# An encoder trunk laid out feature by token: x resident, two token groups, contiguous weight tiles through a ring, and the 31-tap convolution as four concurrent 32-column matmuls

## Chip, cores, metric

The kernel runs on the 8 cores of one Trainium2 chip. Each core does half of one prompt (2048 of 4096 tokens) and one sample of 32 tokens, with all weights. The metric is device time of the slowest core in microseconds (us). In some executions one die (cores 0 to 3 or 4 to 7), sometimes both, showed a lower granted TensorE clock, and the time was longer: one run of the kernel before took 3632.04 us with all eight cores at 0.794 to 0.799, where its fast runs took 3263 to 3300.

## The reference, cut to what matters

```python
D_MODEL, D_INNER, CHUNK, MLP_BLOCK = 1024, 2048, 64, 128
for i in range(DEPTH):                      # four layers, each with its own mixer
    shift, scale, gate = ada_modulation(c, w_ada[i], b_ada[i])
    h = rms_norm(x, g_norm[i]) * (1.0 + scale) + shift
    # kind 0: u, v, z = split(h @ w_in_a);  v = layer_norm(gelu(v))     (gelu on u too)
    #         y = u * chunk_mlp_mix(v, w_s_a, b_s_a)    mixes positions in blocks of 128
    # kind 1: bg, cg, hv, z = split(h @ w_in_b);  y = bg * conv3(cg * hv)
    # kind 2: a, ag, z = split(h @ w_in_c);  y = silu(layer_norm(conv31(a * sigmoid(ag)) + b))
    # kind 3: pv, z = split(h @ w_in_d);  y = (pool(pv) - pv) @ w_pool_d (per group) * scale
    out = (y * silu(z)) @ w_out             # 2048 -> 1024
    x = x + gate * out
return rms_norm(x, g_final), v_rows, conv_b_new, conv_c_new, pool_new
```

The convolutions are depthwise and causal; a core needs some tokens ahead of its half (the halo), and the last rows of each mixer's input are outputs too.

## The kernel before

x lies token by feature (128 tokens on the partitions). h, the input of every projection, lies feature by token. So each layer normalises a block of 128 tokens, transposes it on TensorE and moves it out of PSUM:

```python
def h_post(bi, bl, lt):
    ...
        for kc in range(8):
            dstp = ptA[:, kc, 0:n] if kc < 4 else ptB[:, kc - 4, 0:n]
            ins = h.transpose(out=dstp, in_=xn[:, kc * 128:(kc + 1) * 128], identity=identb[0:n, 0:n])
    ...
    for kc in range(4):        # VectorE: scale and shift while leaving PSUM
        s.op("dve", lambda h, kc=kc: h.tensor_scalar(out=hT[:, kc, c0:c0 + n], in0=ptA[:, kc, 0:n], ...
    for kc in range(4, 8):     # ScalarE: the other half
        s.op("act", lambda h, kc=kc: h.activation(out=hT[:, kc, c0:c0 + n], in_=ptB[:, kc - 4, 0:n], ...
```

The tokens of a core (2176 with halo, and the sample) are worked off in three passes through all four layers, each with its own load of every weight; tiles of 256 columns come out of row-major weights in 1 KB runs:

```python
ST_DEFS = [
    dict(b0=0, nb=6, ncols=768, ep=768, sample=False),
    dict(b0=6, nb=6, ncols=768, ep=768, sample=False),
    dict(b0=12, nb=5, ncols=704, ep=640, sample=True),
]
...
def fetch_in(l, col0):         # one of 16 slots of 1 MB of f32, kept as bf16
    s.dma("pool", "rs%d" % i, v, w_in[l].rearrange("(kc p) n -> p kc n", p=128)[:, :, col0:col0 + 256], ...
```

conv31 builds 28 diagonal 128 x 128 matrices per chunk of 128 channels on GpSimd and runs 28 full matmuls over the shifted input; three taps are left to ScalarE and VectorE:

```python
dg = ...                                    # diag(w[k]) for 28 taps
for (c0, n, b, bo) in nts:                  # 512 and 256 columns
    for k in range(NTD, 31):
        ins = h.matmul(bank(b)[:, bo:bo + n], lhsT=dg[:, k - NTD, :], rhs=G[:, c0 + k:c0 + k + n], start=(k == NTD), stop=(k == 30))
```

The v stage of layer 0 works off 128 tokens at a time: projection (front), LayerNorm statistics, vn (the normalised v, by ScalarE), mixing matmuls and 16 evictions from PSUM (back). The evictions are cut in two, with the statistics of the next block between them:

```python
    evac(0, 8)
    return lambda: evac(8, 16)
...
for bi, bl in enumerate(blocks):
    ctx = v_front(bi, bl)
    tail = v_back(*prevb) if prevb is not None else None
    v_stats(bi, bl, ctx)
    if tail is not None:
        tail()
```

Of the kernel before, what the change touches and what calls it, by code (L numbers as in the profile page):

```python
# [13 lines left out]
EPS = 1e-6  # L14

class Sched:
# [11 lines left out]
    def _deps(self, eng, reads, writes):  # L28
        waits = {}

        def add(sv):
            if sv is None:
                return
            sname, v = sv
            if v > waits.get(sname, 0):
                waits[sname] = v

        for k in reads:
            r = self.res.get(k)
            if r is not None:  # L40
                add(r[0])
        for k in writes:
            r = self.res.get(k)
            if r is not None:
                add(r[0])
                for sname, v in r[1].items():
                    add((sname, v))
        out = []
        for sname, v in waits.items():
            if self.seen[eng].get(sname, 0) >= v:  # L50
                continue
            self.seen[eng][sname] = v
            out.append((sname, v))
        return out
# [10 lines left out]
    def op(self, eng, fn, reads=(), writes=()):  # L65
        ro = getattr(self, "ring_out", None)
        if ro:
            for k in reads:
                ro.discard(k)
# [76 lines left out]
def build_program():  # L146
    nc = bass.Bass("TRN2", target_bir_lowering=False)

# [6 lines left out]
    xp = din("xp", [2176, D])  # L155
    xsm = din("xsm", [32, D])
    st_b = din("st_b", [2, E])
    st_c = din("st_c", [30, E])
    st_d = din("st_d", [15, E])
    cvec = din("cvec", [2, D])  # L160
    maskc_d = din("maskc", [128, 1])
    invc_d = din("invc", [128, 64])
    w_ada = din("w_ada", [4, D, 3 * D])
    b_ada = din("b_ada", [4, 3 * D])
    g_norm = din("g_norm", [4, D])
    w_in = [din("w_in_a", [D, 3 * E]), din("w_in_b", [D, 4 * E]), din("w_in_c", [D, 3 * E]), din("w_in_d", [D, 2 * E])]
    w_out = [din("w_out_a", [E, D]), din("w_out_b", [E, D]), din("w_out_c", [E, D]), din("w_out_d", [E, D])]
    prm9 = din("prm9", [9, E])
    w_conv_c = din("w_conv_c", [31, E])
    w_s_a = din("w_s_a", [8, 128, 128])  # L170
    b_s_a = din("b_s_a", [8, 128])
    w_pool = din("w_pool_d", [4, 512, 512])
    g_final = din("g_final", [1, D])
    ln_a_gb = din("ln_a_gb", [2, E])

    yp = dout("yp", [2048, D])
    ysm = dout("ysm", [32, D])
    vrows = dout("vrows", [32, E])
    o_cb_p = dout("cb_p", [2, E]); o_cb_s = dout("cb_s", [2, E])
    o_cc_p = dout("cc_p", [30, E]); o_cc_s = dout("cc_s", [30, E])  # L180
    o_pd_p = dout("pd_p", [15, E]); o_pd_s = dout("pd_s", [15, E])

    s = Sched(nc)
    TOTAL = 53000
    big = nc.alloc_sbuf_tensor("big", [128, TOTAL], F32)
    off = [0]

    def carve(nw):
        v = big[:, off[0]:off[0] + nw]
        off[0] += nw  # L190
        assert off[0] <= TOTAL, off[0]
        return v

    def v3(v, a):
        return v.rearrange("p (a b) -> p a b", a=a)

    X = v3(carve(6 * 1024), 6)
    XS = X[:, 5, :]
    hT = v3(carve(3072).bitcast(BF16), 8)
    ysT_raw = carve(6144)  # L200
    ysT = v3(ysT_raw.bitcast(BF16), 16)
    AUX_raw = carve(6400)
    AUX = v3(AUX_raw.bitcast(BF16), 16)
    RING = carve(16 * 1024)
    Traw = [carve(800) for _ in range(4)]
    gateP = [carve(1024), carve(1024)]
    gateS = carve(1024)
    dscr = [carve(128), carve(128)]
    scTb = v3(carve(8).bitcast(BF16), 8)
    gf_bc = carve(1024)  # L210
    biasT = v3(carve(2048), 16)
    biasT_s = v3(carve(512), 16)
    WsT = v3(carve(512).bitcast(BF16), 8)
    WsT_s = v3(carve(128).bitcast(BF16), 8)
    identb = carve(64).bitcast(BF16)
    identf = carve(128)
    onesf = carve(128)
    onesb = carve(64).bitcast(BF16)
    prmT = v3(carve(16 * 9), 16)
    wccT = v3(carve(16 * 32), 16)  # L220
    stT = v3(carve(16 * 48), 16)
    hist = v3(carve(16 * 48), 16)
    outS = v3(carve(16 * 48), 16)
    gnT = v3(carve(32), 8)
    badaT = v3(carve(96), 24)
    cT = v3(carve(16), 8)
    scT = v3(carve(16), 8)
    modT = carve(4 * 48)
    gsT = carve(4 * 16)
    stat = carve(64)  # L230
    maskc = carve(1)
    invc = carve(64)
# [7 lines left out]
    PS = nc.alloc_psum_tensor("ps", [128, 4096], F32)  # L240

    def bank(b):
        return PS[:, b * 512:(b + 1) * 512]

    def bk(*bs):
        return ["bk.%d" % b for b in bs]

    def Tf(i, n=800):
        return Traw[i][:, 0:n]

    def Tb(i, n=1600):
        return Traw[i].bitcast(BF16)[:, 0:n]

    def Tk(*idx):
        return ["T.%d" % i for i in idx]

    Tcat = big[:, Traw[0].offset - big.offset:Traw[0].offset - big.offset + 3200] if False else None

    t0_off = 6 * 1024 + 1024 + 3072 + 6144 + 6400 + 16 * 1024
    stage = big[:, t0_off:t0_off + 3200]  # L260
    Tpair01 = big[:, t0_off:t0_off + 1600]

    s.op("pool", lambda h: h.memset(identf, 0.0), writes=["identf"])
    s.op("pool", lambda h: h.affine_select(out=identf, in_=identf, pattern=[[-1, 128]], compare_op=ALU.not_equal,
                                           fill=1.0, base=0, channel_multiplier=1), reads=["identf"], writes=["identf"])
    s.op("dve", lambda h: h.tensor_copy(out=identb, in_=identf), reads=["identf"], writes=["identb"])
    s.op("dve", lambda h: h.memset(onesf, 1.0), writes=["onesf"])
    s.op("dve", lambda h: h.memset(onesb, 1.0), writes=["onesb"])
    s.op("dve", lambda h: h.memset(stat[:, 0:63], 0.0), writes=["stat_init"])
    s.op("dve", lambda h: h.memset(stat[:, 63:64], -0.5), writes=["neghalf"])  # L270
    s.op("dve", lambda h: h.memset(hist.rearrange("p a b -> p (a b)"), 0.0), writes=["hist"])
    s.dma("sp", "su_m", maskc, maskc_d, writes=["maskc"])
    s.dma("sp", "su_i", invc, invc_d, writes=["invc"])
    s.dma("sp", "su_g", gf_bc, g_final.partition_broadcast(128), writes=["gf_bc"])

    def load_rows_T(src, R, C, dst3, dkey, rp=32):
        nch = C // 128
        s.dma("sp", "su_st", stage[0:R, 0:C], src, writes=Tk(0, 1, 2, 3))
        pst = v3(bank(0)[:, 0:nch * rp], nch)

        def f(h):
            ins = None
            for c in range(nch):
                ins = h.transpose(out=pst[:, c, 0:R], in_=stage[0:R, c * 128:(c + 1) * 128], identity=identf[0:R, 0:R])
            return ins
        s.op("pe", f, reads=Tk(0, 1, 2, 3) + ["identf"], writes=bk(0))
        s.op("dve", lambda h: h.tensor_copy(out=dst3[:, :, 0:R], in_=pst[:, :, 0:R]), reads=[], writes=bk(0) + [dkey])

    load_rows_T(cvec, 2, D, cT, "cT")
    load_rows_T(g_norm, 4, D, gnT, "gnT")  # L290
    load_rows_T(b_ada, 4, 3 * D, badaT, "badaT", rp=4)
    load_rows_T(prm9, 9, E, prmT, "prmT")
    load_rows_T(w_conv_c, 31, E, wccT, "wccT")
    load_rows_T(st_b, 2, E, stT[:, :, 0:2], "stT")
    load_rows_T(st_c, 30, E, stT[:, :, 2:32], "stT")
    load_rows_T(st_d, 15, E, stT[:, :, 32:47], "stT")
    s.op("act", lambda h: h.activation(out=scT.rearrange("p a b -> p (a b)"), in_=cT.rearrange("p a b -> p (a b)"), func=AF.Silu),
         reads=["cT"], writes=["scT"])

    wsI = v3(stage[:, 0:1024], 8)  # L300
    s.dma("sp", "su_st", wsI, w_s_a.rearrange("g i j -> i g j"), writes=Tk(0, 1, 2))
    ps_w = v3(PS[:, 0:1024], 8)

    def f_ws_s(h):
        ins = None
        for g in range(8):
            ins = h.transpose(out=ps_w[0:32, g, 0:32], in_=wsI[0:32, g, 0:32], identity=identf[0:32, 0:32])
        return ins
    s.op("pe", f_ws_s, reads=Tk(0, 1, 2) + ["identf"], writes=bk(0, 1))
    s.op("dve", lambda h: h.tensor_copy(out=WsT_s[0:32, :, :], in_=ps_w[0:32, :, 0:32]), reads=[], writes=bk(0, 1) + ["WsT_s"])  # L310
    s.op("dve", lambda h: h.memset(wsI[0:64, :, 64:128], 0.0), reads=[], writes=Tk(0, 1, 2))

    def f_ws(h):
        ins = None
        for g in range(8):
            ins = h.transpose(out=ps_w[:, g, :], in_=wsI[:, g, :], identity=identf)
# [719 lines left out]
```

## Time and profile before

| | before |
|---|---|
| time, median of 3 | 3263.55 us (3263.26 to 3263.99) |
| cores in the profiled run | 3211.7 to 3272.4 us, clock 0.917 to 0.926 |
| matmuls on TensorE | 17058, busy 82% of the span |

The lines that the prediction rests on are quoted in it below. Three more views are needed for the comparison. First the waits of TensorE (who waited on which line, for whom; us in total, times, longest):

```profile
PE ps L547 <- ACT big L531: 126.2, 32, 18.2
PE ps L390 <- DMA big<-w_ada: 52.0, 7, 13.9
...
PE ps L672 <- ACT big L621: 18.8, 9, 2.3
```

L547 are the transposes of the norm, waiting for ScalarE's statistics and scaled rows: 126 us, the largest single item. L390 are the conditioning matmuls, waiting for weights. L672 are the mixing matmuls of the v stage: they wait 18.8 us for ScalarE (L621, its GELU) and, by a line not shown, 32.3 us for VectorE's evictions (L678).

Second, VectorE in one block of that stage. L678 are evictions, L631 to L643 the statistics (columns: start, us, engine, line, operation, output and inputs, shapes, count, and in brackets the idle time before it):

```profile
1301.06 1.26 DVE L678 SCALAR_TENSOR_TENSOR big<-ps,big 128x128 bf16<-128x128 f32 x3
1302.24 0.15 DVE L631 TENSOR_TENSOR big<-big 128x1 f32<-128x1 f32 x1
...
1304.25 0.16 DVE L643 SCALAR_TENSOR_TENSOR big<-big 128x1 f32<-128x1 f32 x1 [0.80 <-POOL big L641]
1304.33 3.54 DVE L678 SCALAR_TENSOR_TENSOR big<-ps,big 128x128 bf16<-128x128 f32 x8
```

The statistics stand between two halves of the evictions, so the second eight evictions run while ScalarE makes vn. From one vn to the next (1304.50 to 1314.88) a block takes 10.4 us.

### The profile page before, as it was taken

The page shows a single profiled execution, that of the slowest core. Times are in us where ns is not written, and L with a number is a line of the kernel's source. Part 1 is how long each engine was busy: PE and PEld are TensorE (multiplying, and loading weights), DVE is VectorE, ACT ScalarE, POOL GpSimd, SP SyncE. Part 2 cuts the span into 40 slices and gives each one's busy share as a digit, 9 for nine tenths or more (in the row PEclk, how much of TensorE's full clock was granted, in tenths as well). Part 3 has the DMA queues.
Part 4 walks back from the last instruction along what each step waited for, and adds up shares of the span by engine and source line. Part 5 has one row for each costly group of instructions (what it writes and reads, how often), then busy time and mean ns, then how long its engine had stood idle before and what let it go on. Part 6 is the DMA issues. An engine that isn't in the chain of part 4 may idle for free.

```text
span 3272.4 us, 45441 instructions; the slowest of 8 cores (3211.7 to 3272.4 us)
## 1 busy us (share of the span) xinstructions
PE 2683.3 (82%) x17058; PEld 1626.0 (50%) x17291; DVE 1499.7 (46%) x2529; ACT 979.4 (30%) x1414; POOL 641.4 (20%) x510
## 2 busy tenths in 40 slices
PE   1466888877998884788998998896688997999798
PEld 1344455444664543554655565453554654665454
DVE  0341244423665662424543566473423553567364
ACT  0531321221125315424223114423524224114421
POOL 1021021021641100201102461110111102263010
PEclk9987988878999987899999999998899998999898
DMA  9169499289113923678729504544093947803451
GB/s 124 48 74 151 60 134 144 32 103 150 31 14 41 127 44 79 74 108 95 112 27 123 84 1 52 78 69 107 13 167 44 148 52 90 118 1 46 65 78 37
DMA packets 389018, 257.24 MB, mean 79 GB/s; under 512 B 8164, under 2 KB 359396, under 8 KB 388522
## 3 DMA queue, kind: packets, MB, share of 16 engines
q0 software_dynamic: 381888, 232.81, 56.1%
q1 hardware_dynamic: 6915, 21.52, 1.9%
q8 instruction: 140, 2.29, 0.3%
q14 instruction: 75, 0.61, 0.1%
HBM read 477.53 MB, written 9.55 MB: 149 GB/s over the span
## 4 chain that ended last, share of the span: by engine, by line
PE 62%; DMA 13%; DVE 11%; issue 7%; ACT 5%; another core or an unknown queue 1%; POOL 1%; DVEq 0%; ACTq 0%; SPq 0%; POOLq 0%
PE ps L465 28%; PE ps L943 16%; PE ps L815 13%; DMA big<-w_in_a 4%; DMA big<-w_ada 2%; DMA big<-w_in_b 2%; ACT big L555 2%; DVE big L678 2%; PE ps L921 1%; DMA big<-w_in_c 1%; DVE big L856 1%; ACT big L526 1%; PE ps L613 1%; DVE big L895 1%; DVE big L903 1%
## 5 line engine op out<-in xcount | busy, mean ns | idle before, releaser
L465 PE MATMUL ps<-big 128*128 128x256 bf16 (+2 forms) x8317 | 1358.0, 325 | 136.6 <-ACT big L555 33.2
L465 PEld LDWEIGHTS ps<-big 128*128 128x128 bf16 x8448 | 825.1, 100 | 663.0 <-issue 189.4
L943 PE MATMUL ps<-big 128*128 128x512 bf16 (+1 forms) x2256 | 517.5, 388 | 52.4 <-issue 47.9
L815 PE MATMUL ps<-big 128*128 128x256 bf16 (+3 forms) x2682 | 419.9, 316 | 3.5 <-DVE big L788 3.2
L943 PEld LDWEIGHTS ps<-big 128*128 128x128 bf16 (+1 forms) x2304 | 227.3, 100 | 330.1 <-issue 77.8
L815 PEld LDWEIGHTS ps<-big 128*128 128x128 bf16 x2688 | 255.1, 97 | 161.5 <-issue 5.5
L768 POOL TENSOR_TENSOR big<-big 128x3584 bf16<-128x3584 bf16 x42 | 259.5, 6178 | 143.3 <-PE ps L815 143.3
L807 DVE SCALAR_TENSOR_TENSOR big<-big 128x768 f32<-128x768 bf16 (+1 forms) x96 | 224.6, 2340 | 92.5 <-ACT big L804 87.2
L102 POOL DMA_DIRECT2D big<-w_in_b x96 | 84.1, 904 | 504.7 <-PE ps L465 280.5
L526 ACT ACTIVATE big<-big 128x1024 bf16<-128x1024 f32 x72 | 75.9, 1054 | 349.3 <-DVE big L525 327.2
L714 DVE TENSOR_TENSOR big<-big 128x768 bf16<-128x768 bf16 (+1 forms) x96 | 52.5, 547 | 236.2 <-ACT big L712 235.9
L547 PE MATMUL ps<-big 128*128 128x128 bf16 (+1 forms) x576 | 52.2, 245 | 130.3 <-ACT big L531 126.2
L952 DVE TENSOR_TENSOR big<-ps,big 128x1024 f32<-128x1024 f32 x72 | 87.9, 1220 | 154.8 <-PE ps L943 154.8
L824 ACT ACTIVATE big<-big 128x768 bf16<-128x768 bf16 (+1 forms) x48 | 39.6, 825 | 367.7 <-DVE big L820 367.7
L613 PE MATMUL ps<-big 128*128 128x256 bf16 (+1 forms) x1152 | 138.5, 285 | 11.4 <-ACT big L555 5.4
L712 ACT ACTIVATE big<-ps 128x768 bf16<-128x768 f32 (+1 forms) x96 | 75.9, 792 | 236.7 <-PE ps L465 213.9
L102 POOL DMA_DIRECT2D big<-w_in_c x72 | 63.2, 917 | 399.1 <-PE ps L547 183.5
L785 DVE TENSOR_TENSOR big<-big,ps 128x768 bf16<-128x768 f32 (+1 forms) x48 | 44.7, 931 | 205.4 <-ACT big L783 149.2
L555 ACT ACTIVATE big<-ps,big 128x128 bf16<-128x128 bf16 (+1 forms) x288 | 127.3, 450 | 36.2 <-PE ps L547 14.0
L613 PEld LDWEIGHTS ps<-big 128*128 128x128 bf16 (+1 forms) x1152 | 116.9, 102 | 30.8 <-issue 12.6
L551 DVE TENSOR_SCALAR big<-ps,big 128x128 bf16<-128x128 bf16 (+1 forms) x288 | 96.1, 341 | 73.3 <-PE ps L547 49.3
L678 DVE SCALAR_TENSOR_TENSOR big<-ps,big 128x128 bf16<-128x128 f32 (+1 forms) x288 | 99.2, 344 | 60.2 <-PE ps L672 32.0
(142 smaller groups left out, 2294.8 us busy)
## 6 DMA issues: line engine op xcount, KB each, us to landing
big<-w_in_b POOLq DMA_DIRECT2D x96, 512.0 KB, 25.8
big<-w_in_a POOLq DMA_DIRECT2D x72, 512.0 KB, 29.6
big<-w_in_c POOLq DMA_DIRECT2D x72, 512.0 KB, 44.7
big<-w_ada POOLq DMA_DIRECT2D x48, 512.0 KB, 37.6
big<-w_in_d POOLq DMA_DIRECT2D x48, 512.0 KB, 6.4
big<-w_out_a POOLq DMA_DIRECT2D x24, 512.0 KB, 45.0
big<-w_out_b POOLq DMA_DIRECT2D x24, 512.0 KB, 11.9
big<-w_out_c POOLq DMA_DIRECT2D x24, 512.0 KB, 27.9
```

What stands on the lines that cost most here:

```text
L102: h.dma_start(out=out, in_=in_, **kw).then_inc(dsm, 16)
L465: ins = h.matmul(bank(b)[:, bo:bo + n], lhsT=wv[:, kc, ci * 128:(ci + 1) * 128], rhs=hT[:, kc, c0:c0 + n], start=(kc == 0), stop=(kc == 7))
L526: s.op("act", lambda h: h.activation(out=junkv[0:n, :], in_=xt, func=AF.Square, scale=1.0 / 32, accum_out=stat[0:n, so:so + 1]), reads=[bl ...
L551: s.op("dve", lambda h, kc=kc: h.tensor_scalar(out=hT[:, kc, c0:c0 + n], in0=ptA[:, kc, 0:n], scalar1=gst[:, kc, sq:sq + 1], scalar2=mvt[: ...
L555: s.op("act", lambda h, kc=kc: h.activation(out=hT[:, kc, c0:c0 + n], in_=ptB[:, kc - 4, 0:n], func=AF.Identity, scale=gst[:, kc, sq:sq + ...
L613: ins = h.matmul(bank(q // 2)[0:n, (q % 2) * 256:(q % 2) * 256 + 256], lhsT=hT[:, kc, c0:c0 + n], rhs=wv_slots[q][1][:, kc, :], start=(kc ...
L678: s.op("dve", lambda h, cc=cc: h.scalar_tensor_tensor(out=ysT[:, cc, c0:c0 + n], in0=mps[:, cc, :], scalar=prmT[:, cc, 7:8], in1=bt[:, cc, ...
L768: s.op(eng, lambda h: h.tensor_tensor(out=dg, in0=id_bc, in1=w_bc, op=ALU.mult), reads=["identb", "wccT"], writes=dkeys)
L807: s.op("dve", lambda h, G=G, acc=acc, c=c, k=k: h.scalar_tensor_tensor(out=acc[:, 0:ncols], in0=G[:, k:k + ncols], scalar=wccT[:, c, k:k + 1],
L815: ins = h.matmul(bank(b)[:, bo:bo + n], lhsT=dg[:, k - NTD, :], rhs=G[:, c0 + k:c0 + k + n], start=(k == NTD), stop=(k == 30))
L943: ins = h.matmul(bank(2 * p + hf)[0:n, :], lhsT=ysT[:, ec, c0:c0 + n], rhs=wo[ec // 2][1][:, ec % 2, hf * 512:(hf + 1) * 512], start=(ec = ...
L952: s.op("dve", lambda h, p=p, n=n, tmp=tmp, gsrc=gsrc: h.tensor_tensor(out=tmp, in0=PS[0:n, p * 1024:(p + 1) * 1024], in1=gsrc[0:n, :], op= ...
```

## The change

The intent: x lies feature by token and stays in SBUF from the first load to the last store, so no transposes are needed; the norm's sums over features become matmuls with a column of ones. Two groups of tokens (1074 and 1056 columns) alternate through every layer, so that the norm of one can be computed in the output projection of the other. Weights are put into 1 MB tiles by the host, 8 KB contiguous per partition, and run through a ring of 8 slots whose order is known beforehand. The core of the diff (the whole is over 1800 lines; cuts are marked by dots):

```diff
-    ST_DEFS = [
-        dict(b0=0, nb=6, ncols=768, ep=768, sample=False),
-        ...
+HALO = 50
+NPA = 1024
+NCOL = (HALO + NPA, NPA + 32)
+WT = (NCOL[0] // 3, NCOL[1] // 3)          # three PSUM banks of 358 or 352 columns
+NSLOT = 8
 ...
+    def pump():                            # the next tile as soon as a slot is free
+        while free and order is not None and nxt["i"] < len(order):
+            ...
+            s.dma("pool", "rs%d" % i, ring[:, i * 2048:(i + 1) * 2048], w_dram[spec[0]][spec[1]], writes=["rs.%d" % i])
 ...
+        def stats(d):                      # sums of squares: three packed matmuls with 32 columns of ones
+            for q in range(3):
+                ins = h.matmul(PSB[32 * q:32 * q + 32, 6, 0:W], lhsT=onesD, rhs=hT[:, d, c0 + q * W:c0 + (q + 1) * W], ...
+        def bc(): ...                      # 1/rms back on 128 partitions: TensorE, then a ScalarE copy
+        def apply(d): ...                  # x * (1/rms), scale and shift: VectorE
 ...
+            for ps, c, n, nb, smp in pieces(g, sl, WT[g], 0):      # end of an output chunk: x += gate * out, one op
+                s.op("dve", lambda h, ...: h.scalar_tensor_tensor(out=xv, in0=ps, scalar=gate[:, 16 + d, smp:smp + 1], in1=xv, ...
+            for fn in hooks.get(d, ()):    # a piece of the other group's norm after each output chunk
+                fn()
```

conv31: the 128 channels of a chunk are written to HBM and read back four times as 32 channels x 4 shifts, so that a 128 x 32 matrix does four taps of 32 channels. Eight of them do 32 taps (the last is zero), and four groups of 32 channels go into four column groups of the array:

```diff
-                        for (c0, n, b, bo) in nts:
-                            for k in range(NTD, 31):
-                                ins = h.matmul(bank(b)[:, bo:bo + n], lhsT=dg[:, k - NTD, :], rhs=G[:, c0 + k:c0 + k + n], ...
+            s.dma("sp", "gw%d" % (c % 4), g_dram[c % 4], G, reads=gk, writes=["gd.%d" % (c % 4)])
+            ...
+            for sft in range(4):
+                s.dma("sp", "gr%d_%d" % (ci, sft), R[32 * sft:32 * sft + 32, :, 0:RW],
+                      bass.AP(src.tensor, src.offset + sft, [[GW, 32], [32 * GW, 4], [1, RW]]), ...
+            ...
+                for b in range(8):
+                    for n in range(3):
+                        for j in range(4):
+                            ins = h.matmul(PSB[32 * j:32 * j + 32, 3 * sl + n, 0:WC], lhsT=wd[:, b, j, :],
+                                           rhs=R[:, j, 4 * b + n * WC:4 * b + (n + 1) * WC], start=(b == 0), stop=(b == 7), ...
```

And the v stage, where all 16 evictions and a product with u now stand ahead of the next statistics, with one vn buffer in place of two:

```diff
-                    evac(0, 8)
-                    return lambda: evac(8, 16)
+            for cc in range(16):
+                s.op("dve", lambda h, cc=cc: h.scalar_tensor_tensor(out=mt[:, cc, 0:no], in0=PSB[:, 4 + cc // 4, ...
+            s.op("dve", lambda h: h.tensor_tensor(out=ysT[:, :, oc:oc + no], in0=ysT[:, :, oc:oc + no], in1=mt[:, :, 0:no], op=ALU.mult), ...
 ...
+        for bi in range(nb):
+            front(bi)
+            if bi:
+                back(bi - 1)
+            stats(bi)
+        back(nb - 1)
```

## The prediction

> **What bounds the kernel now.** I read the page first (busy time, slices), then stretches of the second of its three passes over the tokens (768 columns, 1253 to 2254 us), then the TensorE timeline inside two of them.
>
> ```profile
> PE 2683.3 (82%) x17058; PEld 1626.0 (50%) x17291; DVE 1499.7 (46%) x2529; ACT 979.4 (30%) x1414; POOL 641.4 (20%) x510
> ...
> PE   1466888877998884788998998896688997999798
> HBM read 477.53 MB, written 9.55 MB: 149 GB/s over the span
> ```
>
> TensorE is the only engine near full; its slices are thin at the start. The second fence cuts one pass into stages (columns: us, busy time per engine, granted clock, DMA share, GB/s).
>
> ```profile
> 0.00:420.00 420.00, 226.44 (x1817) 154.62 (x1835) 105.19 (x314) 123.11 (x184) 65.81 (x84) 0.90 0.70 91
> 1253.00:1280.00 27.00, 6.38 (x50) 4.92 (x51) 8.74 (x33) 22.29 (x45) 0.00 (x0) 0.50 0.31 72
> 1280.00:1357.00 77.00, 55.17 (x480) 46.21 (x480) 36.78 (x128) 39.70 (x48) 14.40 (x19) 0.83 0.13 14
> ...
> 1509.00:1684.00 175.00, 169.49 (x1019) 102.66 (x1039) 92.30 (x128) 41.20 (x50) 19.64 (x24) 0.99 0.78 101
> 1684.00:1741.00 57.00, 46.53 (x237) 22.37 (x243) 23.47 (x48) 26.93 (x49) 11.83 (x14) 0.90 0.21 24
> 1741.00:1828.00 87.00, 86.48 (x516) 52.38 (x526) 27.47 (x47) 14.46 (x17) 14.09 (x18) 0.97 1.24 156
> 1828.00:1987.00 159.00, 156.42 (x950) 93.51 (x965) 92.55 (x52) 27.50 (x33) 87.19 (x15) 1.00 0.07 13
> ```
>
> The projections of layer 1 (1509 to 1684) and conv31 (1828 to 1987) are TensorE back to back. Norm and transposes (1253 to 1280), the v stage of layer 0 (1280 to 1357) and the ends of the output projections (in 1684 to 1741) are not. The first 420 us hold setup plus layer 0 up to its output projection; the same layer takes some 230 us in the second pass, so setup and weight waits cost about 200 us, and the rest of the first pass some more.
>
> The third fence is the TensorE timeline in conv31: 56 matmuls (28 taps, 512 and 256 columns), then the statistics of the chunk before, no gap.
>
> ```profile
> 1866.76 9.30 PE L815 MATMUL ps<-big 128*128 128x512 bf16 x56
> ...
> 1876.11 0.38 PE L831 MATMUL ps<-big 128*128 128x512 bf16 x1
> ...
> 1886.33 9.29 PE L815 MATMUL ps<-big 128*128 128x512 bf16 x56
> ```
>
> 28 x 768 = 21,504 columns take 9.35 us: 2.30 columns per ns. Layer 1: 64 chunks x 8 x 768 = 393,216 columns in 171 us, 2.30 again. I price all dense TensorE work at this rate.
>
> [...] With plain tiling the trace has load-plus-matmul pairs (the 2-column conditioning matmuls) 26 ns apart, so four pairs need 104 ns to issue, less than the 152 ns that 358 columns stream. [...]
>
> **The change part by part.** Columns: before 2240 (2160 after layer 0), after 1074 + 1056 = 2130. All instruction counts below are from the code.
>
> - Projections in. Layer 0 u and z: 32 chunks x 8 x 2130 = 545k columns, 237 us. Layer 1: 64 chunks, 474. Layer 2 a, gate, z: 48 chunks, 356. Layer 3: 237; its pooled map 16 x 4 x 2130 = 136k, 59. These move little: same columns, same rate.
> - Output projections: 8 x 16 x 2130 = 273k columns, 118.5 us each, 474 for four. Before, one layer's takes about 50 us per pass (1684 to 1736), with transposes and a 5 to 10 us tail for the next norm: some 600 in all. Norm now comes from a ones matmul and is computed for the other group inside the output phase, so the tails and the three 27 us norm stretches go, about 200 us off the path.
> - Conv31: 28 diagonal 128-column matmuls become 8 x 4 of 32 columns. Before, in the TensorE timeline from its first to its last matmul: 142 + 156 + 143 us for three passes. After: 16 chunks x 8 x 2160 columns x 4 = 1,106k columns, 481 us if serial, 120 if ideal[...]. Statistics 68k columns packed by three: 12. Off: about 275 us. GpSimd's 42 diagonal builds of 6.18 us vanish with it; they were off the path. In return each chunk makes a trip through HBM: 0.29 MB out, four 0.28 MB reads back, two chunks (about 20 us) ahead of its use. With 1 MB of weights per 12 us that is some 200 GB/s of HBM traffic; the stretch 1741 to 1828 moved 156 GB/s into SBUF from f32 weights, about 300 of HBM. It should stay hidden.
> - v stage of layer 0, the one part that I expect to be worse. Before, a block takes 9.9 us (from one start of its matmuls to the next, 1298.9 to 1308.9): half of the 16 evictions, then the statistics, then the other half. Now all 16 and a product run ahead of the next statistics, with one vn buffer. Durations from the timeline 1299 to 1321: 16 evictions at 0.44 us spacing 7.1, product 1.3, statistics to vn 2.3, vn 2.1, first mixing matmuls 0.3: 13.1 us per block against 7.9 of TensorE. 18 blocks, two short: 230 us against 215 before.
> - Weights: 132 tiles x 2 + 48 = 312 of 1 MB in place of 444, in 8 KB instead of 1 KB runs. The tiles of before landed in 6 us when alone (w_in_d 6.4). A 256-column tile now feeds 2 x 8 x 1065 columns, 7.4 us: 142 GB/s needed, so projections should not starve.
>
> Sum of the dense parts: 237 + 230 + 474 + 356 + 237 + 59 + 474 + 152 + 12 = 2231 us.
>
> Additions, estimates of mine: start (8 MB of conditioning weights and 4.7 MB of x at about 200 GB/s, then the first norm) 80; the final norm of the second group 24 (8 x 1.28 us on VectorE, reciprocal, broadcast, last stores); v rows of the sample with two loads in line 12; twelve conditioning blocks at 3 us 36; ring waits around those of layer 1 18; norm statistics and broadcasts on TensorE 24; sixteen phase changes at 2 us 32; the tail of layer 2 (LayerNorm finish, then four applies of 3.5 us of which the first 12 chunks of the output projection hide 5.6) 24; lower clock and loads at the edges of the v stage 25. Sum 275. Total **2506 us**; I say 2510, **23% less**.
>
> Check from the other side: 3264 - 200 (start) - 275 (conv) - 200 (norm, transposes, tails) - 50 (columns and waits of the first pass) = 2540.
>
> VectorE: layer 1 needs about 8.2 us per chunk (one scalar op 0.8, two fused 1.3, three tensor ops 1.3 to 1.6) against 14.8 of TensorE; layer 3, window 16, 7.4 against 7.4 before its pooled map. It nearly ties there, nowhere leads.
>
> **Rivals.**
> 1. The four 32-column matmuls run one after another, or each waits for its own load. For: nothing before shows packing[...]. [...] Serial adds 329 us: 2840, still 13% faster.
> 2. Two accumulators of three banks instead of four pairs: every eviction now stands close to TensorE's next write. For: one late VectorE or ScalarE op stops the array, and idle stretches halve its clock (0.50 in 1253 to 1280). Against: a chunk streams for 3.7 us and its eviction takes 1.1 to 1.6. If a quarter of the 352 chunks lost 1.5 us, 132 us: 2640.
> 3. The HBM round trip or the small ring (8 tiles against 16) starves TensorE: conv waits 5 us in 32 chunks, 160 us: 2670. Against: the slack above.
> 4. Startup is not shortened, all cores asking HBM at once: +80 us.
>
> **Range and chances.** Errors are more often upward: rivals 1 (one in eight) and 2 or 3 in part (one in three). Downward: packing near ideal gives 30, additions half as large 100. 80% range 2400 to 2700. Even rivals 1, 3 and 4 together give about 3080, 6% under before; so faster 0.96, same 0.03, slower 0.01.
>
> **What would show it.** Right: one conv chunk of TensorE at 4 to 6 us; PE share near 87%; v stage about 115 us per group, paced by VectorE; layer 1 about 235 us per group; first dense projection at about 80 us; HBM read some 380 MB with the trips. Wrong: conv chunks near 15 us (rival 1), waits of TensorE for evictions all over (2), waits for the scratch reads or weight tiles in layers 1 and 2 (3). The prediction fails upward if two of these hold, or if a stage that I took as TensorE's turns out VectorE's; downward if the additions overlap.

Four of its numbers need their source. The 152 us of conv31 in the sum are the estimate, between the 120 of an ideal packing and the 481 of a serial one; that much packing was not shown, the trace of the kernel before has none at all. The 275, 329 and 30 us and the sum follow from it. The 152 ns for 358 columns lie between the 109 ns for 256 columns and the 216 for 512 at which the matmuls of conv31 follow each other in the kernel before; in the changed kernel those of the projections (358 columns, 1445 to 1453 us) start 150 to 162 ns apart, 154 in the median. The 1.28 us of a VectorE op on 1074 columns continue the 893 ns for 704 columns and 958 for 768 of the kernel before (L858, f32); the changed kernel has 1.27 to 1.28 (L709, L841). The 200 GB/s of the start was an estimate; 218 came.

## More of the kernel before

Third, the queue of the weights (packets, MB, share of 16 engines' span):

```profile
q0 software_dynamic: 381888, 232.81, 56.1%
```

## The result, and the profile after

| | before | after |
|---|---|---|
| time, median of 4 | 3263.77 us (3263.26 to 3264.65) | 2508.19 us (2507.80 to 2508.91) |
| ratio of fast runs | 1 | 0.7686 (95%: 0.7673 to 0.7698) |
| cores in the profiled run | 3211.7 to 3272.4 us, clock 0.917 to 0.926 | 2495.2 to 2507.3 us, clock 0.958 to 0.960 |

A ratio here is the mean time of one kernel's fast runs over the mean of the other's fast runs of the same rounds, so it is not quite the ratio of the medians that are quoted. The outputs are correct, as in all experiments below. Executions in which one die ran at a lower clock are left out of the means.

The page of the changed kernel:

```profile
PE 2197.7 (88%) x16767; PEld 1359.5 (54%) x16767; DVE 1113.0 (44%) x1804; ACT 648.9 (26%) x723; POOL 178.6 (7%) x337
...
PE   1596599775799999999999999989998899998995
...
q0 software_dynamic: 45072, 163.86, 39.4%
HBM read 374.91 MB, written 18.73 MB: 157 GB/s over the span
```

TensorE is thin only in the first eleven slices (start and layer 0) and in the last one. Five stretches of core 4 (columns: window and its length, then busy us and count of TensorE, weight loads, VectorE, ScalarE, GpSimd, then granted clock, DMA share, GB/s):

```profile
0.00:70.00 70.00, 10.84 (x98) 4.70 (x98) 7.32 (x20) 13.62 (x15) 9.37 (x22) 1.00 0.99 218
70.00:162.00 92.00, 68.80 (x384) 38.96 (x385) 20.76 (x48) 17.27 (x16) 4.29 (x8) 0.91 0.42 82
162.00:289.00 127.00, 82.06 (x437) 39.13 (x434) 61.82 (x185) 59.73 (x82) 9.78 (x18) 0.86 0.16 24
...
763.00:1006.00 243.00, 240.12 (x1642) 152.93 (x1641) 123.40 (x156) 36.61 (x37) 23.58 (x44) 1.00 0.60 95
...
2034.00:2193.00 159.00, 148.72 (x964) 93.08 (x961) 104.90 (x156) 42.12 (x41) 10.75 (x20) 1.00 0.38 67
```

In order: start (loads above all: DMA share 0.99), the u projection of the first group, its v stage (TensorE busy 82 of 127 us), layer 1 of the first group (240 of 243), layer 3 of one group (149 of 159).

TensorE's timeline in conv31 (L782 the convolution of a chunk, L798 the statistics, L439 the projections):

```profile
1441.12 3.85 PE L782 MATMUL ps<-tmp 128*32 128x358 bf16 x96
1444.80 0.32 PE L798 MATMUL ps<-ysT,onesE 128*32 128x358 bf16 x3
...
1445.20 7.53 PE L439 MATMUL ps<-hT,ring 128*128 128x358 bf16 x48
```

96 matmuls of 358 columns take 3.85 us; at one every 152 ns, the spacing within one column group in serial_cols below, they would take 14.6. In the instruction records the four of a group start 1 to 5 ns apart, and the next group some 150 ns later; from the first start to that of the statistics it is 3.68 us, so four run in the time of one. Against the 56 matmuls in 9.3 us of before, a chunk now has 1074 columns in place of 768.

VectorE in one block of the v stage (L633 evictions, L637 the product, L600 to L605 the statistics):

```profile
205.00 1.73 DVE L633 SCALAR_TENSOR_TENSOR tmp<-ps,cst_sb,tmp 128x128 bf16<-128x128 f32 x4 [3.20 <-PE ps L625]
...
212.48 1.23 DVE L637 TENSOR_TENSOR ysT<-ysT,tmp 128x2048 bf16<-128x2048 bf16 x1
213.62 0.21 DVE L600 TENSOR_SCALAR stat<-stat 128x1 f32<-128x1 f32 x1
...
215.55 0.16 DVE L605 SCALAR_TENSOR_TENSOR stat<-stat 128x1 f32<-128x1 f32 x1 [0.80 <-POOL stat L604]
```

All 16 evictions and the product come first. vn follows on ScalarE at 215.86 (the one before it was at 201.94), and VectorE idles 3.2 us until the mixing matmuls have vn. The block takes 13.92 us from vn to vn, against 10.4 before.

The waits of TensorE:

```profile
PE ps L625 <- ACT tmp L606: 88.1, 18, 12.7
PE ps L342 <- DMA ring<-w_ada: 46.5, 3, 27.3
PE ps L439 <- DVE tmp L633: 14.8, 1, 14.8
PE ps L782 <- DMA tmp<-gscr: 14.6, 5, 3.8
PE ps L439 <- DVE ysT L847: 12.8, 8, 2.6
PE ps L439 <- DVE hT L420: 11.5, 10, 3.5
```

Norm is down to 11.5 us (hT, L420) and 9.3 us at the two exposed norms (L407 on L399) from 126. The mixing matmuls (L625) now wait 88 us for vn (L606): the new largest wait. Before, they waited 18.8 for ScalarE and 32.3 for evictions. The reads of conv31 (gscr) cost 14.6 us in all.

### Where the 765 us came from

The starts and ends of the stages are read from TensorE's timeline (before on core 0, changed on core 4; each column adds up to the profiled span). "In" is everything of a layer ahead of its output projection; for before, three passes are added.

| stage | before | after | difference |
|---|---|---|---|
| start, and layer 0 in | 801.1 | 639.3 | -161.8 |
| layer 1 in | 542.6 | 479.0 | -63.6 |
| layer 2 in, with conv31 | 897.8 | 526.9 | -370.9 |
| layer 3 in, with pooled map | 346.1 | 320.1 | -26.0 |
| four output projections, with the next norm | 669.7 | 513.0 | -156.7 |
| after the last output projection | 15.1 | 29.0 | +13.9 |
| sum | 3272.4 | 2507.3 | -765.1 |

In layer 2 conv31 with its statistics was 448.6 us before (three stretches, each up to the next projection). After, it is 32 chunks of 4.08 us (1441.12 to 1445.20), 131 us, of which the convolution's matmuls are some 3.9 us each, 125 us.

### The profile page after: what moved, and what is told of

It reads as the page before. It is cut to its first block, busy times and chain, and to the rows that moved or that the text cites. A ratio compares the mean times of both kernels' runs of the same rounds, so it can differ in the third digit from the quotient of the medians.

```text
span 2507.3 us, 41303 instructions; the slowest of 8 cores (2495.2 to 2507.3 us)
## 1 busy us (share of the span) xinstructions
PE 2197.7 (88%) x16767; PEld 1359.5 (54%) x16767; DVE 1113.0 (44%) x1804; ACT 648.9 (26%) x723; POOL 178.6 (7%) x337
## 3 DMA queue, kind: packets, MB, share of 16 engines
q0 software_dynamic: 45072, 163.86, 39.4%
q1 hardware_dynamic: 30240, 65.97, 10.4%
HBM read 374.91 MB, written 18.73 MB: 157 GB/s over the span
## 4 chain that ended last, share of the span: by engine, by line
PE 70%; DVE 13%; DMA 7%; issue 4%; ACT 4%; POOL 1%; DVEq 1%; SPq 0%; ACTq 0%; POOLq 0%
PE ps L439 63%; PE ps L782 4%; DVE tmp L633 3%; DVE tmp L951 3%; DMA ring<-w_ada 2%; DMA gscr<-tmp 2%; ACT tmp L606 2%; DMA tmp<-gscr 1%; DMA ring<-w_in_a 1%; DVE tmp L958 1%; ACT tmp L931 1%; PE ps L574 1%; DVE hT L416 1%; DVE xb_sb L490 1%; DVEq L101 0%
## 5 line engine op out<-in xcount | busy, mean ns | idle before, releaser
L439 PE MATMUL ps<-hT,ring 128*128 128x358 bf16 (+1 forms) x8448 | 1311.8, 317 | 57.5 <-DVE tmp L633 14.8
L439 PEld LDWEIGHTS ps<-hT,ring 128*128 128x128 bf16 x8448 | 827.2, 98 | 537.3 <-issue 81.4
L439 PE MATMUL ps<-ysT,ring 128*128 128x352 bf16 (+1 forms) x3072 | 476.2, 315 | 21.6 <-DVE ysT L847 12.8
L439 PEld LDWEIGHTS ps<-ysT,ring 128*128 128x128 bf16 x3072 | 298.5, 98 | 199.0 <-issue 32.0
L574 PE MATMUL ps<-ring,hT 128*128 128x512 bf16 (+1 forms) x576 | 145.0, 416 | 10.2 <-DMA ring<-w_in_a 8.4
L782 PE MATMUL ps<-tmp 128*32 128x358 bf16 (+1 forms) x3072 | 130.5, 327 | 14.6 <-DMA tmp<-gscr 14.6
L633 DVE SCALAR_TENSOR_TENSOR tmp<-ps,cst_sb,tmp 128x128 bf16<-128x128 f32 (+2 forms) x288 | 98.0, 340 | 84.7 <-PE ps L625 51.9
L782 PEld LDWEIGHTS ps<-tmp 128*32 128x32 bf16 x3072 | 83.3, 99 | 59.9 <-issue 24.2
L951 DVE TENSOR_TENSOR tmp<-tmp 128x1088 f32<-128x1088 f32 (+5 forms) x80 | 102.8, 1285 | 5.1 <-DVE tmp L951 0.2
L625 PE MATMUL ps<-WsT,tmp 128*128 128x128 bf16 (+2 forms) x288 | 24.3, 253 | 88.1 <-ACT tmp L606 88.1
L490 DVE SCALAR_TENSOR_TENSOR xa_sb<-ps,modT,xa_sb 128x1074 f32<-128x1074 f32 x32 | 42.7, 1335 | 122.8 <-PE ps L439 122.8
L702 DVE SCALAR_TENSOR_TENSOR tmp<-tmp,cst_sb 128x1074 f32<-128x1074 f32 (+1 forms) x64 | 85.1, 1329 | 7.1 <-DVE tmp L699 0.5
L439 PE MATMUL ps<-tmp,ring 128*128 128x358 bf16 (+1 forms) x384 | 61.9, 319 | 13.2 <-DVE ysT L910 9.3
L625 PEld LDWEIGHTS ps<-WsT,tmp 128*128 128x128 bf16 (+1 forms) x288 | 21.0, 117 | 95.9 <-issue 95.9
```

The lines of the kernel that those rows point to most:

```text
L439: ins = h.matmul(PSB[:, 3 * sl + n, 0:W], lhsT=lw, rhs=rh[:, n * W:(n + 1) * W], start=(first and k == 0), stop=(last and k == len(pairs) ...
L490: s.op("dve", lambda h, ps=ps, xv=xv, smp=smp, d=d: h.scalar_tensor_tensor(out=xv, in0=ps, scalar=gate[:, 16 + d, smp:smp + 1], in1=xv, op ...
L574: ins = h.matmul(PSB[0:n, nq, :], lhsT=hT[:, kh * 4 + kk, hc:hc + n], rhs=vw[nq * 2 + kh][:, kk, :], start=(kh == 0 and kk == 0), stop=(kh ...
L625: ins = h.matmul(PSB[:, 4 + bank, i * 128:i * 128 + no], lhsT=vn[:, cc * 128:(cc + 1) * 128], rhs=WsT[0:n, cc // 2, w0:w0 + no], start=Tru ...
L633: s.op("dve", lambda h, cc=cc: h.scalar_tensor_tensor(out=mt[:, cc, 0:no], in0=PSB[:, 4 + cc // 4, (cc % 4) * 128:(cc % 4) * 128 + no], sc ...
L702: s.op("dve", lambda h, p=p, a=a, c=c, wd=wd, k=k: h.scalar_tensor_tensor(out=a[:, 0:wd], in0=p[:, k:k + wd], scalar=prmT[:, c, k:k + 1], ...
```

## The experiments

Theory: TensorE's columns set the time; the gain is packing of conv31, norm taken off the path, and a start with less in it; the v stage gives some back because VectorE's order holds up vn. Rivals: (1) the four column groups do not really overlap; (2) evictions stand too close to TensorE's next write and pace it; (3) the HBM trip of conv31, or the small ring, starves TensorE. Every experiment changes the changed kernel; "+" and "-" in us are against it.

### serial_cols: the column group outermost

```diff
-                for b in range(8):
+                for j in range(4):
                     for n in range(3):
-                        for j in range(4):
+                        for b in range(8):
```

The same 96 matmuls per chunk, with the same operands; the four that could run side by side are just no longer neighbours.

> The changed kernel with the conv31 matmuls of a chunk issued column tile by column tile (all 24 of one 32-column tile, then the next), instead of four neighbours in turn; the same 96 instructions, the same result. If the gain of conv31 is that four neighbouring tiles run side by side, a chunk's matmuls go from the 3.85 us of the trace to 96 x 152 ns = 14.6 us; 32 chunks x 10.7 = +344 us, about 2850. Rival: the array overlaps the tiles by itself, or the gain is only fewer columns: within 30 us of the changed kernel.

One run, the profiled one: 2791.73 us, +283 (the other three slow, at 2838 to 3182). It isn't quite undisturbed: cores 4 and 5 have spells at a granted clock of 0.81, 147 us in all, and took 2788 and 2790 us. The six other cores took 2766 to 2772, as did the undisturbed cores of the slow runs, against at most 2507 in the changed kernel: +265 is the better figure. TensorE's timeline:

```profile
1468.82 12.51 PE L782 MATMUL ps<-tmp 128*32 128x358 bf16 x93
...
1489.18 12.51 PE L782 MATMUL ps<-tmp 128*32 128x358 bf16 x93
```

A chunk takes about 12.9 us with its last three matmuls and its statistics, not 14.6: within one column group they are 152 ns apart, but at the three seams between groups the last few of one overlap with the first of the next. The records show it best at the end of a chunk: the statistics, issued last but in other column groups, start at 1481.03, and the last three matmuls of the convolution at 1481.17 to 1481.48. So packing comes from the order of issue. From chunk to chunk it is 20.36 us in place of 11.54; 8.8 us x 32 = 282, less the 15 us of waits for the reads, which are gone, accounts for the time. It also says what the gain is made of: in this order conv31 takes 32 x 12.9 = 413 us with its statistics, little less than the 448.6 of before. The HBM trip, the shifted copies and the smaller matrices pay only through the four groups at once. Rival 1 falls.

### norm_after: the norm of the other group after the output projection

```diff
-            out_phase(l, g, hooks, late)
+            out_phase(l, g, {}, late)
+            for d in sorted(hooks):
+                for fn in hooks[d]:
+                    fn()
```

> The changed kernel with the norm of the other group computed after the output projection instead of inside it; same work. Theory (the two groups are what hides the norm): each of 7 norms then puts squares 9, statistics and root 5, broadcast 3 and the apply-paced first projection 13 us on the path, about 30 less a little overlap: 7 x 25 to 30 plus the half clock after each gap, +180 to +230 us, about 2710. Rival (norm was cheap anyway, and the gain of the layout is elsewhere): under +60 us.

One fast run: 2665.11 us, +157 (the three others slow; the cores of their undisturbed die took 2654 to 2666 too). Seven norms ahead of a projection are moved out, some 20 us each, and the final one of the first group, which makes the end 43 us long in place of 29. The waits of TensorE:

```profile
PE ps L439 <- DVE hT L420: 80.7, 59, 3.8
PE ps L407 <- ACT tmp L399: 54.8, 10, 5.8
```

They stood at 11.5 and 9.3. Part of the cost is clock: after each of seven output projections the records show 24 to 27 us at half clock, and the mean fell from 0.958 to 0.925. The expectation, 180 to 230 us, was a little high: the squares on ScalarE still ran early (in layer 0 at 359 to 367 us, beside the output projection of 357 to 417). That the 157 us equal the 156.7 us of the output projections in the table above is chance: what that row lost holds the transposes too. That the norm lies beside the other group's output projection is what the alternating groups are for, and it is worth this much.

### row_weights: weights row-major in HBM again

```diff
-            s.dma("pool", "rs%d" % i, ring[:, i * 2048:(i + 1) * 2048], w_dram[spec[0]][spec[1]], writes=["rs.%d" % i])
+            wsrc, wn = w_src(spec[0], spec[1])      # strided view: 1 KB runs (512 B for output tiles)
+            s.dma("pool", "rs%d" % i, v3(ring[:, i * 2048:(i + 1) * 2048], wn), wsrc, writes=["rs.%d" % i])
```

> The changed kernel with the weights left in their row-major layout in HBM, so a tile is read in runs of 1 KB (projections in) or 512 B (projections out) in place of 8 KB; ring and order unchanged. Theory (transfers are hidden, 7.4 us of matmuls per tile): DMA share up, time within 2% (start and v-stage edges +10 to +40 us). Rival (contiguous tiles are what lets 8 slots in place of 16 feed TensorE): +5% or more, TensorE waiting for weight tiles in layers 1 to 3.

Three fast runs: 2540.98 to 2542.85 us, ratio to before 0.7764 (0.7714 to 0.7814), +33 us or 1.3%. The weights' queue:

```profile
q0 software_dynamic: 377872, 163.86, 56.5%
```

The same bytes in short runs keep the DMA engines busy for 56.5% of the span in place of 39.4%, almost the share of before, and yet nearly all of it stays hidden. TensorE's wait for the conditioning weights, nearly all at the start, grew from 46.5 to 62.5 us, that for layer 0's weights from 8.7 to 17.0, and a wait of 9.4 us for layer 1's appeared: 34 us together. So contiguous tiles are worth 1.3%, half of it at the start, where little hides a load: in the changed kernel TensorE is busy 10.8 of those 70 us, at a DMA share of 0.99. After the start (70 us) TensorE waits only 10.5 us for tiles of the ring in the changed kernel, so by the waits the part of rival 3 that blames the ring falls; the number of slots was not varied.

### v_half and v_half2: the evictions in two halves again

```diff
+            def tail():
+                evac(8, 16)
+                s.op("dve", ... ysT * mt ...)
+            evac(0, 8)
+            return tail
 ...
             front(bi)
-            if bi:
-                back(bi - 1)
+            tail = back(bi - 1) if bi else None
             stats(bi)
-        back(nb - 1)
+            if tail is not None:
+                tail()
+        back(nb - 1)()
```

The first build, v_half, ran on no chip: evictions of the next block wrote the scratch tile mt while nothing ordered them after the product that reads it.

> The changed kernel with the v stage ordered as before: 8 of 16 evictions, the statistics of the next block, then the other 8 and the product. Theory (the stage is paced by the loop eviction, product, statistics, vn, mixing matmuls on VectorE and ScalarE): the period of 13.9 us falls to about 11 (VectorE alone has 7.5 + 1.3 + 1.5 us a block, and ScalarE 7), 16 full blocks x 2.9 = -46 us, 2462; range -30 to -60. Rival (the stage is paced by TensorE, its matmuls at half clock): within 10 us of the changed kernel.

v_half2 is the same with the product also recorded as a writer of mt, which gives that order.

> The refused v-stage order, mended: the product now also marks its scratch tile as written, so that the next block's evictions are ordered after it. Same expectation: theory (loop over VectorE and ScalarE) -46 us on the changed kernel, between -30 and -60, the period of a block near 11 us in place of 13.9; rival (TensorE at half clock paces the stage) within 10 us.

Three fast runs: 2464.65, 2465.23, 2469.04 us; ratio to before 0.7519 (0.7474 to 0.7565). Against evict_twice of the same batch, which is as fast as the changed kernel (below, mean 2510.7), that is -44 us. VectorE's timeline (L634 the evictions here):

```profile
224.85 1.72 DVE L634 SCALAR_TENSOR_TENSOR tmp<-ps,cst_sb,tmp 128x128 bf16<-128x128 f32 x4 [0.17 <-DVE tmp L634]
226.48 0.20 DVE L600 TENSOR_SCALAR stat<-stat 128x1 f32<-128x1 f32 x1
...
228.40 0.16 DVE L605 SCALAR_TENSOR_TENSOR stat<-stat 128x1 f32<-128x1 f32 x1 [0.80 <-POOL stat L604]
228.52 1.73 DVE L634 SCALAR_TENSOR_TENSOR tmp<-ps,cst_sb,tmp 128x128 bf16<-128x128 f32 x4
```

The statistics stand after eight evictions, and the other eight run beside vn. From one second half (here 228.52) to the same place of the block before (217.85), it is 10.7 us in place of 13.9, close to the 10.4 of the kernel before. The waits of TensorE:

```profile
PE ps L625 <- ACT tmp L606: 42.7, 18, 9.1
PE ps L625 <- DVE tmp L634: 22.0, 15, 15.0
```

88.1 us have become 42.7, and a wait of 22.0 for VectorE. Of that, 15.0 are one wait, behind the sample's v rows, which stood elsewhere (L439 on L633, 14.8) in the changed kernel; 7 are new. So what the v stage gives back is the order of VectorE's work, as predicted.

### evict_twice: two evictions of layer 1 done twice

The copy of the second projection (CG) and the SiLU of z of layer 1, both on ScalarE from PSUM, are each issued twice, so that PSUM should come free later and ScalarE has more to do.

```diff
-                s.op("act", lambda h, sl=sz_, c=c: h.activation(out=v3(ysT[:, c, 0:NC], 3), ...
+                for _ in range(2):
+                    s.op("act", lambda h, sl=sz_, c=c: h.activation(out=v3(ysT[:, c, 0:NC], 3), ...
```

> The changed kernel with two of the four evictions of layer 1 (the copy and the SiLU of ScalarE) done twice, the same result: +1.06 us on 64 evictions, 68 us of ScalarE work. Theory (with 3.7 us of matmuls per accumulator the two slots leave slack): within 10 us of the changed kernel. Rival (two slots of three banks are tight): +30 to +70 us.

Two fast runs, 2509.40 and 2511.91 us; ratio 0.7652 (0.7610 to 0.7694): no change. The stretch of layer 1:

```profile
763.00:1006.00 243.00, 240.17 (x1642) 153.17 (x1639) 123.53 (x156) 71.21 (x69) 23.65 (x45) 1.00 0.60 95
```

ScalarE's busy time went from 36.6 to 71.2 us and TensorE's did not move. Rival 2 falls for layer 1. For layer 3 it was not tested; there TensorE shows some 10 us of idle time in 159 us.

### trip_twice: the four reads of conv31's trip done twice

```diff
-            for sft in range(4):
+            for sft in (0, 1, 2, 3, 0, 1, 2, 3):
```

> The changed kernel with the four reads of conv31's trip through HBM done twice in a row into the same place: 36 MB more of reads and about 6 us more of latency per chunk. Theory (20 us from the write to the use, of which about 13 are taken): +0 to +40 us, waits of conv31 for the reads from 15 us to at most 60. Rival (the trip is at its limit): every chunk waits 5 us or more, +160 us.

Two fast runs, 2679.91 and 2670.94 us; ratio 0.8154 (0.8082 to 0.8226). That is +165 against evict_twice of the same batch: the expectation, 0 to 40 us, was wrong, and the rival's +160 came. (In the first of the two, the profiled one, die 1 had spells at a clock of 0.81; with the second alone it is +160.) The wait of TensorE for the reads:

```profile
PE ps L782 <- DMA tmp<-gscr: 144.1, 27, 10.5
```

and SyncE's own queue (start, us in which the queue issued, count):

```profile
1442.40 8.08 SPq L122 DMA_DIRECT2D tmp<-gscr  x8
1450.57 0.39 SPq L122 DMA_DIRECT2D gscr<-tmp  x1
```

In the changed kernel four reads take 2.7 us of that queue. Eight take 8.1, and the write of the next chunk stands behind them in the same queue. The records say why it is so long: each of the second four reads goes into the place of one of the first four, and leaves the queue some 0.06 us after that one has landed (1446.33, then 1446.39, and so on). So for part of the 8.1 us the queue waits, and the edit puts a second landing behind the first; it adds latency, and not bytes alone. So more reads may cost in two ways: the reads themselves, or the order of the queue.

### changed_again, trip_act, trip_twice_act: the write from ScalarE's queue

trip_act issues the write to HBM from ScalarE's queue, so that it doesn't stand behind reads; trip_twice_act does that with the reads doubled. changed_again is the changed kernel on the same chip.

```diff
-            s.dma("sp", "gw%d" % (c % 4), g_dram[c % 4], G, reads=gk, writes=["gd.%d" % (c % 4)])
+            s.dma("act", "gw%d" % (c % 4), g_dram[c % 4], G, reads=gk, writes=["gd.%d" % (c % 4)])
```

> The changed kernel unaltered, as the base of this batch on its chip: within 0.5% of 2508.

> The changed kernel with the write of conv31's trip issued from ScalarE's queue; the reads stay on SyncE's. In the trace a trip takes about 16 of 22 us, of which the write 5 to 8, and on SyncE's queue a chunk's write stands behind the reads of the chunk before. Theory Q (that one queue, in order, sets the pace): the waits of conv31 for the reads fall from 15 to under 5 us, time 0 to -15. Theory T (the transfers themselves take the time): waits stay near 15.

> The doubled reads (2671, 144 us of waits) with the write on ScalarE's queue. Theory Q: the writes now overlap the reads of the chunk before, one chunk holds SyncE's queue some 10 us in place of 17, under the 11.5 us of a chunk; waits fall to under 50 us, time about 2560. Theory T: waits stay above 120, time 2650 or more.

| kernel | fast runs, us | ratio to before (95%) |
|---|---|---|
| changed_again | 2507.41, 2512.63, 2510.92 | 0.7662 (0.7604 to 0.7721) |
| trip_act | 2500.93, 2516.80 | 0.7653 (0.7586 to 0.7720) |
| trip_twice_act | 2596.50, 2596.01 | 0.7920 (0.7860 to 0.7980) |

The wait of TensorE for the reads in trip_twice_act:

```profile
PE ps L782 <- DMA tmp<-gscr: 82.4, 23, 11.9
```

With single reads the other queue changes nothing that these runs could tell; the wait for the reads is 11.1 us against 14.3 in changed_again, not the "under 5" of theory Q. With doubled reads it takes about half of the cost away: +87 (2596.3 against 2508.9) in place of +165. So neither theory holds alone: about half was the order in SyncE's queue. The other half stays with the reads. Their second landing in line is the likely part, by the records above; issue, bytes and landing were not separated by a run.

### combined and combined_act: what the findings make together

combined is v_half2 with three more edits: the two loads and the arithmetic for the sample's v rows go after the last eviction, with other scratch for z; the setup of the mixing biases is done in three steps within the first projection, in PSUM banks 6 and 7, instead of stopping it; and the squares of the first norm come ahead of the second conditioning block. combined_act also moves the write as above.

```diff
+              def rows_out(): ...
+              deferred.append(rows_out)
 ...
+        for fn in deferred:
+            fn()
-        ZT = [0, 576, 1152, 1728]
+        ZT = [4096, 4672, 5248, 5824]
 ...
-    ADA_AT = {(0, 0): {1: [("mix",)], 8: [(0, 2)]},
+    ADA_AT = {(0, 0): {1: [("mix", 0)], 3: [("mix", 1)], 4: [("mix", 2)], 8: [(0, 2)]},
 ...
     ada(0, 0)
-    ada(0, 1)
     ...                                    # squares and statistics of the first norm
     rstd()
+    ada(0, 1)
     bc()
```

> Four waits of the changed kernel's trace taken off at once: the v order of the run before (-46), the v rows of the sample moved after the last eviction with the z tiles in another place (-15, the wait ahead of the z projections of the second group), the setup of the mixing bias in two steps on the two spare banks with its weights asked for two steps earlier (-15), the squares of the first norm ahead of the second conditioning block (-10). If the waits are independent and on the path the sum is about -85 us on the changed kernel, 2420; if they hide behind each other or behind weight tiles, -50 or less.

> The combined kernel (2418) with the write on ScalarE's queue: theory Q -5 to -15, about 2408; theory T within 4 us of it.

combined: all four runs fast, 2417.19 to 2421.97 us, ratio 0.7373 (0.7353 to 0.7393), -92 against evict_twice of its batch. combined_act: all four fast, 2412.76 to 2414.68 us, ratio 0.7363 (0.7328 to 0.7398), -97 against changed_again of its batch. The two ratios can't be told apart. Of the 92 us, 44 are v_half2's; the three further edits give some 47 together (40 expected) and were not run one by one. The waits of TensorE in combined:

```profile
PE ps L630 <- ACT tmp L609: 41.7, 17, 9.1
PE ps L342 <- DMA ring<-w_ada: 32.0, 3, 28.1
```

The wait for v rows (14.8) is no longer among the largest, the conditioning weights cost 32.0 in place of 46.5. Both kernels beat the changed one by nearly 4%. The ratios of v_half2, combined, evict_twice and trip_twice to before rest on little: only two of the kernel before's seven runs on that chip were fast, and the verdict on record for these four is "unclear". Their comparison with evict_twice, in the same batch, doesn't need those runs.

## Why the prediction was right

It said 2510 us, and 2508 came. The sum was right because its errors cancelled. With the prediction's terms booked by stage (twelve conditioning blocks by where they stand: two at the start, four in layer 0, six in layer 1; the phase changes all with the output projections, which is a choice of this table):

| stage | predicted | measured | error |
|---|---|---|---|
| start (80 + 6) | 86 | 70.0 | -16 |
| layer 0 in (237 + 230 + 12 + 12 + 25) | 516 | 569.3 | +53 |
| layer 1 in (474 + 18 + 18) | 510 | 479.0 | -31 |
| layer 2 in (356 + 152 + 12 + 24) | 544 | 526.9 | -17 |
| layer 3 in (237 + 59) | 296 | 320.1 | +24 |
| output projections (474 + 24 + 32) | 530 | 513.0 | -17 |
| end | 24 | 29.0 | +5 |
| sum | 2506 | 2507.3 | +1 |

- **Columns at 2.30 per ns: right.** 48 matmuls of 358 columns in 7.53 us are 2.28. Layer 1, pure TensorE, took 243 and 236 us for the two groups with its conditioning blocks, where "about 235" was said. The 18 us for waits on the ring did not come: no ring wait of layer 1 is among the large ones.
- **Conv31: the mechanism right, the size too cautious.** 152 us were the estimate, which no trace had shown; 125 came, and by the starts (3.68 us a chunk) 118, the prediction's ideal (120); the statistics were said to be 12 and are 32 x 0.4 = 13. serial_cols shows the mechanism.
- **Norm and tails off the path: right**; about 200 us were said. The output projections with their norms and transposes lost 157 of 669.7 ("some 600" in the prediction); the rest of the norm is booked with layer 0, where the table can't separate it. norm_after shows that the place of the norm matters, +157.
- **v stage worse: right, and still too small.** 13.1 us per block were said, 13.92 came. The 9.9 us said for before are misread: the two starts that it names are 10.0 apart, and from vn to vn it is 10.4. The pieces, from the timeline: gap after vn until the first eviction 0.97 (0.3 said), 16 evictions 7.48 (7.1), product 1.14 (1.3), statistics 2.24 (2.3), vn 2.09 (2.1). With the fill of the first block and the short blocks, which are not shorter in this chain (the last wait of L625 was 12.7 us), 126 + 138 = 264 us came for 230. v rows: 14.8 us, 12 said.
- **Start: about right in length, wrong in what follows it.** The first dense projection began at 70 us, but that stretch took 92 us where 61 would do: TensorE was busy 69 of it, paced by the norm's applies and stopped once by the mixing biases. Combined took most of this away.
- **Layer 3 "nearly ties": right in kind**, but no term was booked for it: +24 us. That the ~10 us of idle time in one group's stretch are VectorE and ScalarE is read from the waits; no experiment was made.
- **Contiguous tiles hidden: right within 1.3%**, from row_weights.
- **The HBM trip "should stay hidden": right in outcome, wrong in the margin.** The prediction argued with bytes (200 GB/s asked) and with two chunks, some 20 us, of slack. In the trace the glu of a chunk ends at 1431.1, the write has landed at 1439.6, the reads at 1447.4, and the chunk is used at 1452.7: 16 of 22 us were gone. Doubled reads, each waiting for the first to land, overran it (+165). HBM traffic was estimated well (374.91 MB read, 380 said) and was not what counts.

The gain of resident x and fewer columns (2240 to 2130 per pass over a layer) was not isolated by an experiment; what the table gives to layer 1 (-63.6 us) is the best reading of it and includes waits of before for weights (29.0 us in the waits of TensorE). Nor were the 161.8 us of the start and layer 0 taken apart.

## What to carry to other kernels

Price TensorE's stages in columns at the rate that the trace shows, and then look for the loops that go through two other engines and back. The v stage was such a loop, paced by the order of instructions and not by busy time (TensorE busy 82 of 127 us, VectorE 62, ScalarE 60): moving eight evictions behind the statistics gave 44 us with no work removed. Issue packed tiles as neighbours: a chunk's 96 matmuls and its statistics took 4.08 us that way, and about 12.9 when the four of a group were not adjacent. The trip of conv31 was hidden by slack in time, of which 16 of 22 us were gone, and doubled reads on the queue that issues it cost 165 us; so measure issue, landing and use in the trace before counting on such slack. The 200 GB/s on which the prediction relied said nothing of that margin.

## What these runs show of packing, clock, packets and queues

- Packing: in a stream of 24 groups of four, 96 matmuls of 358 columns took 3.85 us against 14.6 at 152 ns each, 3.8 for four tiles, and 3.68 from the first start to the next matmul, almost 4; the same 96 with the four of a group not adjacent took about 12.9 with the statistics (serial_cols).
- Between packed and plain matmuls: from the last packed statistics (start 1444.95, three within a few ns) to the next 128-column projection at 1445.20 it is 0.25 us, and from the last projection to the next packed group 0.245 (1440.87 to 1441.12): some 0.1 more than the 0.15 from one projection matmul to the next. It came twice per chunk and is small; what takes the time is not shown.
- Clock: all eight cores ran dense matmuls, with a TensorE 88% busy, and in the profiled run of the changed kernel no core has anything but 1.0 (2202 to 2208 us) and 0.5 (201 to 213 us) among its clock records (mean 0.958 to 0.960). A clock of 0.81 does occur: two profiled runs have spells of it (serial_cols 147 us on cores 4 and 5 alone, whose mean is 0.955 and 0.956 against 0.963 to 0.965 of the others; trip_twice 133 us on these and, at another time, 23 to 36 us on cores 6 and 7), and a whole die near 0.82 is seen (a run of changed_again at 2799 us: 0.82 on one die, 0.958 on the other). What starts it is not shown.
- Packets: with row-major weights (row_weights) the packets averaged 434 B (163.86 MB in 377,872, counted as bf16 in SBUF; twice that in HBM) and took 0.565 x 2541 = 1436 us of the engines' time, against 0.394 x 2507 = 988 us for the same bytes in packets of 3.6 KB: 45% more, of which 33 us showed in the time.
- A queue that also waits: in trip_twice four more reads, each waiting for an earlier one to land, stood ahead of a write and cost 165 us over 32 chunks, and 87 with the write on another engine's queue (trip_twice_act).
